# Dilated attention scores on four row groups of 32, and 512-wide pairs for the dilated chunks of the first layer

## The chip, the cores and the metric

The kernel runs on one core of one Trainium2 chip. Its time is the device time of one execution in microseconds (us); the median of the runs counts. Engines are named as the profile names them: PE (matmuls; PEld loads its weights), DVE (vector), ACT (scalar), POOL, and SP, whose queue issues the weight transfers.

## The reference

Two layers of a decoder trunk over 256 positions and a width of 1024, then a last normalization. Every layer runs one projection of the normalized input and three branches on its columns:

```
proj = hn @ w_in                      # a_q a_k a_v a_g | b_x b_g | c_q c_k c_v c_g
qa, ka = partial_rope(a_q), partial_rope(a_k)     # 8 heads of 64, the first 16 dims rotated
y_a = dilated_attention(qa, ka, a_v) * silu(a_g)  # three patterns: (128,1) (512,4) (2048,16)
y_b = rg_lru(b_x) * silu(b_g)                     # conv of 4, gates, linear recurrence
y_c = stick_breaking(c_q, c_k, c_v) * silu(c_g)   # 4 heads of 64
x = x + concat(y_a, y_b, y_c) @ w_out
```

In the dilated branch a query sees its causal keys, each with a weight that counts in how many patterns it occurs. Per head the scores are thus one 128x128 block (first query tile) and one 128x256 block (second query tile), with an additive mask.

## The kernel before

Activations are kept as two rounded parts, `xh` and `xl`, side by side in `xx`. The weights of a layer come in 18 chunks of 128x2048, two transfers each into `st`; ACT rounds each piece of 512 columns into `whi` (L109) and DVE puts the remainder into `wlo` (L110). A product is three matmul terms: hi by xh, hi by xl, lo by xh. A chunk of 256 output rows is made in two halves of 128 (`proj_b`). In the plain form (`mm3`, L211) each half is 24 matmuls 256 wide, and the two halves share one PSUM bank. In the paired form (chunks named in `PAIRED`, before in layer 1 alone) a half is 8 matmuls 512 wide (hi by xh and xl at once, L332) and 8 matmuls 256 wide (L329) in a PSUM bank of its own; ACT copies the xl half out (`low`, L335) and DVE adds it to the other (L337), which frees the bank.

PSUM has three pools: `pp` with three banks, `s` with four, `y` with one. `st` has five buffers.

Within a layer PE runs in the order in which the program is written; DVE, ACT and the others are ordered by a scheduler when the kernel is built. The order on PE in layer 0, from the stick-breaking queries on: CQ, CK, AQ0 (stick-breaking scores, L443, between its halves), AK0, BX (the convolution's input, with four transposes between its halves), eight more transposes (L463), AQ1 (between its halves `second`: the scores of dilated heads 0 to 3, L497), AK1, CG, twelve transposes of the probabilities (L463), BG (between its halves `third`: the recurrence's gates L557, the products with the values L427, the scores of heads 4 to 7), AG0, AG1, and the output chunks O0 to O3.

`rotate` applies the rotary table to a chunk's 512 columns with four DVE operations of that width (L481 to L484). `dil_scores` issues the fp32 matmuls of four heads, two heads at a time on 64 rows each, and then reads the scores on DVE (mask and minimum, L504). `dil_softmax` is an exponential per block on ACT (L83), a reciprocal (L515) and a scaling (L517) on DVE. `turned` copies transposed blocks from PSUM with ACT (L464, into `wv`, or `pa` and `pb`).

Of the kernel before, what the change touches and what calls it, by code (L numbers as in the profile page):

```python
# [20 lines left out]
NK = D // P  # L21
HD = 64
# [22 lines left out]
PAIRED = ((), (CH_CQ, CH_CK, CH_AQ[0], CH_AK[0], CH_BX, CH_AQ[1], CH_AK[1]))  # L45


@with_exitstack
def trunk_kernel(ctx: ExitStack, tc: tile.TileContext, x, first_x, first, wpack, prm_d, gatew, gains, consts, rope, out):
    nc = tc.nc  # L50
    act, dve, pe, gps = nc.scalar, nc.vector, nc.tensor, nc.gpsimd
# [35 lines left out]
    def v2(a, n=2):  # L87
        return a.rearrange("p (b t) -> p b t", b=n)
# [208 lines left out]
    for l in range(L):  # L297
# [8 lines left out]
        y_half(0)  # L306
# [7 lines left out]
        def proj_b(c, mid=None, to=None, sc=1.0):  # L314
            pair = c in PAIRED[l]
            hi, lo = [a.rearrange("p (k c) -> p k c", c=256) for a in weights(l, c, AHEAD - 1 if mid else AHEAD)]
            if pair:
                flat = None if to is not None else scr(512)
                to = v2(flat) if to is None else to
            else:  # L320
                flat = bank(pp, "pp")
            for b in range(2):
                cs = slice(b * P, b * P + P)
                if pair:
                    ps = bank(pp, "pp")
                    seq = [(0, k) for k in range(NK - 1)] + [(1, k) for k in range(NK)] + [(0, NK - 1)]
                    for i, (is_lo, k) in enumerate(seq):
                        if is_lo:
                            pe.matmul(ps[:, 0:S], lo[:, k, cs], xh[:, k, :], start=False, stop=False,  # L329
                                      skip_group_check=True)  # L330
                        else:
                            pe.matmul(ps, hi[:, k, cs], xx[:, k].rearrange("p h t -> p (h t)"), start=i == 0,  # L332
                                      stop=i == len(seq) - 1, skip_group_check=True)
                    low = wk.tile([P, S], F32, name="low", tag="low", bufs=2)
                    act.activation(low, ps[:, S:2 * S], AF.Copy, scale=sc)  # L335
                    if sc == 1.0:
                        dve.tensor_add(to[:, b, :], ps[:, 0:S], low)  # L337
                    else:
                        dve.scalar_tensor_tensor(to[:, b, :], ps[:, 0:S], sc, low, ALU.mult, ALU.add)
                else:  # L340
                    mm3(flat[:, b * 256:(b + 1) * 256], [lambda k, a=a: a[:, k, cs] for a in (hi, lo)],
                        [lambda k, a=a: a[:, k, :] for a in (xh, xl)], range(NK), True, True)
                if b == 0 and mid:
                    mid()
                    ask(l, c)
            return flat

        def proj_to(dst, c, mid=None, sc=1.0):
            if l > 0 and c in PAIRED[l]:
                proj_b(c, mid, dst, sc)  # L350
            else:
                scaled(dst, proj_b(c, mid), sc)

# [64 lines left out]
        def head(h):  # L418
            return slice((h % 2) * HD, (h % 2) * HD + HD), h // 2, slice(h * HD, (h + 1) * HD)
# [53 lines left out]
            parts[2] = a[:, 768:1024], b[:, 0:128]  # L473
            return parts

        def rotate(ps, tiles, h0, tag):
            dst = tiles[h0] = sb.tile([P, 2, S], F32, name=tag, tag=tag)
            rt_ = rp0 if l == 0 else rp
            cc, ss = [rt_[:, i:i + 1, :].broadcast_to([P, 2, S]) for i in range(2)]
            sw = scr(512)  # L480
            dve.stream_shuffle(sw, ps, SHUF)  # L481
            dve.tensor_mul(dst, v2(ps), cc)
            dve.tensor_mul(v2(sw), v2(sw), ss)
            dve.tensor_add(dst, dst, v2(sw))  # L484

        qT, kT = {}, {}
        prob = {}

        def dil_scores(h0):
            sps = {}  # L490
            for p in (h0, h0 + 2):
                for h in (p, p + 1):
                    sps[h] = bank(at, "s")
                for t, cs in halves:
                    for h in (p, p + 1):
                        hr, hb, _ = head(h - h0)
                        pe.matmul(sps[h][:, cs], qT[h0][hr, hb, t * P:(t + 1) * P], kT[h0][hr, hb, 0:(t + 1) * P],  # L497
                                  start=True, stop=True)
            shifted = {}
            for h in range(h0, h0 + 4):  # L500
                xs = scr(384)
                mn = wk.tile([P, 2], F32, name="mn", tag="mn", bufs=4)
                for t, cs in halves:
                    dve.tensor_tensor_reduce(xs[:, cs], sps[h][:, cs], nmask[:, cs], -0.125, 3e38,  # L504
                                             ALU.add, ALU.min, mn[:, t:t + 1])
                shifted[h] = xs, mn
            return shifted

        def dil_softmax(shifted):
            for h, (xs, mn) in shifted.items():  # L510
                pr = wk.tile([P, 384], F32, name="pr", tag="pr", bufs=4)
                den = wk.tile([P, 2], F32, name="den", tag="den", bufs=4)
                for t, cs in halves:
                    tab(pr[:, cs], xs[:, cs], AF.Exp, bias=mn[:, t:t + 1], scale=-1.0, accum_out=den[:, t:t + 1])
                dve.reciprocal(den, den)  # L515
                for t, cs in halves:
                    dve.tensor_scalar(pr[:, cs], pr[:, cs], den[:, t:t + 1], None, ALU.mult)  # L517
                prob[h] = pr
# [18 lines left out]
        ag = sb.tile([P, 4, S], F32, name="ag", tag="ag")  # L537
        cg = sb.tile([P, 2, S], F32, name="cg", tag="cg")

        def conv(mid):  # L540
# [53 lines left out]
        if l == 0:  # L594
            for i in range(2):
                dve.tensor_mul(rp0[:, i, :], rp[:, i, :], rb)
        rotate(proj_b(CH_AQ[0], sb_scores), qT, 0, "q0")
        rotate(proj_b(CH_AK[0]), kT, 0, "k0")
        sw_t, sw_heads = turned_tile()
        conv(lambda: turned(sw, 0, (0,), sw_t))  # L600
        turned(sw, 0, (1, 2), sw_t)
# [11 lines left out]
        silu(cg, cg_ps)  # L613


        def third():
            lru_gates()
# [7 lines left out]
        lru_scan()  # L625
        emit_y(rt, bg, 0, 2)
        dil_softmax(y_c["s"])
        ps = proj_b(CH_AG)
        table(SIGM)
        silu(ag[:, 0:2, :], ps)  # L630
# [56 lines left out]
def _rope_table():  # L687
    f = np.float32
    pos = np.arange(S, dtype=f)
    inv = f(500000.0) ** (-np.arange(0, 16, 2, dtype=f) / f(16))  # L690
    ang = (pos[:, None] * inv[None, :]).astype(f)
    cos, sin = np.cos(ang).T, np.sin(ang).T
    tab = np.zeros((P, 2, S), f)
    tab[:, 0] = 1.0
    for h in range(2):
        r = h * HD
        tab[r:r + 8, 0] = tab[r + 8:r + 16, 0] = cos
        tab[r:r + 8, 1] = -sin
        tab[r + 8:r + 16, 1] = sin
    return tab  # L700


def _pack_weights(w_in, w_out):
    wp = np.empty((L, NCH, P, 2048), np.float32)
    narrow = ((CH_CV, 3072), (CH_BX, 2048), (CH_BG, 2304), (CH_AG, 1536), (CH_AG + 1, 1792), (CH_CG, 3328),
              (CH_CQ, 2560), (CH_CK, 2816), (CH_AQ[0], 0), (CH_AQ[1], 256), (CH_AK[0], 512), (CH_AK[1], 768))
    yk = (4, 5, 6, 7, 0, 1, 2, 3)
    for l in range(L):
        wi = w_in[l].reshape(NK, P, 3584)
        for h in range(2):  # L710
            wp[l, CH_AV + h] = wi[4 * h:4 * h + 4, :, 1024:1536].transpose(1, 0, 2).reshape(P, 2048)
        for c, col in narrow:
            wp[l, c] = wi[:, :, col:col + 256].transpose(1, 0, 2).reshape(P, 2048)
# [62 lines left out]
```

## Time and profile before

| what | us |
|---|---|
| median of 3 runs (lowest to highest) | 249.79 (249.78 to 250.01) |
| the profiled execution | 248.82 |
| its span, first to last instruction | 246.7 |
| PE busy | 239.0 |
| DVE busy | 196.5 |
| ACT busy | 167.2 |

The profiled execution was 0.97 us shorter than the median, and 2.12 us of it lie outside the span. Positions in the trace are microseconds from the span's start. Layer 0's dilated chunks run from about 39 to 75, layer 1's from about 154 to 190. Rows of the timeline read: start, length, engine, line, operation, outputs and inputs, shape, number of instructions, and in brackets the idle time ahead with what ended it. Rows of the chain read: start, length, engine, tile, line, number.

### The profile page before, as it was taken

How to read it: one execution, taken by the hardware profiler on the slowest of the kernel's cores; microseconds unless marked ns; L12 is line 12 of the kernel's file. 1: busy time of each engine (PE TensorE's matmuls, PEld its weight loads, DVE VectorE, ACT ScalarE, POOL GpSimd, SP SyncE). 2: the span in 40 equal slices, each digit the busy share in tenths (PEclk: the TensorE clock that was granted, in tenths of full speed). 3: DMA queues.
4: the chain of work that ended last, by engine and by line, in shares of the span. 5: the costliest groups of instructions: out<-in, count | busy, mean ns of one | idle time of the engine just before them, and what ended most of it. 6: DMA issues, size and time to landing. Idle time of an engine off the chain costs nothing.

```text
span 246.7 us, 4531 instructions
## 1 busy us (share of the span) xinstructions
PE 239.0 (97%) x1657; PEld 212.1 (86%) x1657; DVE 196.5 (80%) x442; ACT 167.2 (68%) x360; POOL 12.1 (5%) x45
## 2 busy tenths in 40 slices
PE   8999999999999999999999999999999999999990
PEld 4889999999998899878889988889889889987870
DVE  3885699999999799985792766999999987985253
ACT  3778989735947499964662885865498649992142
POOL 0037000001000000000100000000010000000000
PEclk9999999999999999999999999999999999999998
DMA  6989889268447741277157486605553672000022
GB/s 201 404 292 403 342 288 333 96 215 268 134 157 255 258 117 56 85 240 284 74 189 232 142 268 243 200 7 165 161 157 119 197 262 98 0 0 3 0 85 85
DMA packets 13173, 43.89 MB, mean 178 GB/s; under 512 B 1632, under 2 KB 2144, under 8 KB 13152
## 3 DMA queue, kind: packets, MB, share of 16 engines
q1 hardware_dynamic: 12384, 42.30, 51.1%
q10 hardware_dynamic: 576, 0.79, 0.9%
q0 software_dynamic: 192, 0.52, 0.7%
q8 instruction: 13, 0.21, 0.4%
q14 instruction: 8, 0.07, 0.1%
HBM read 42.03 MB, written 1.05 MB: 175 GB/s over the span
## 4 chain that ended last, share of the span: by engine, by line
PE 94%; DMA 2%; DVE 1%; ACT 1%; SPq 0%; issue 0%; ACTq 0%
PE pp L211 51%; PE pp L332 11%; PE s L211 9%; PE pp L329 5%; PE s L169 4%; PE s L463 3%; PE s L497 2%; PE y L427 2%; DMA st<-first 2%; PE pp L169 2%; PE s L443 1%; PE pp L427 1%; PE s L557 1%; PE s L259 1%; DVE xres L668 0%; ACT scr L242 0%
## 5 line engine op out<-in xcount | busy, mean ns | idle before, releaser
L110 DVE TENSOR_TENSOR wlo<-st,whi 128x512 fp32r<-128x512 f32 x132 | 84.1, 683 | 12.8 <-ACT whi L109 12.5
L109 ACT ACTIVATE whi<-st 128x512 fp32r<-128x512 f32 x132 | 73.9, 629 | 28.0 <-PE pp L211 11.8
L211 PE MATMUL pp<-xx,whi 128*128 128x256 f32 x480 | 63.3, 285 | 0.0
L211 PEld LDWEIGHTS pp<-xx,whi 128*128 128x128 f32 x480 | 59.7, 191 | 1.4 <-issue 1.3
L211 PE MATMUL pp<-xx,wlo 128*128 128x256 f32 x240 | 33.7, 283 | 0.0
L211 PEld LDWEIGHTS pp<-xx,wlo 128*128 128x128 f32 x240 | 30.9, 192 | 0.0
L332 PE MATMUL pp<-xx,whi 128*128 128x512 f32 x112 | 29.3, 396 | 0.0
L332 PEld LDWEIGHTS pp<-xx,whi 128*128 128x128 f32 x112 | 20.1, 189 | 4.1 <-ACT scr L83 0.3
L77 ACT ACT_TABLE_LOAD x13 | 16.7, 1283 | 1.9 <-PEq L769 1.7
L83 ACT ACTIVATE pr<-scr,mn 128x128 f32<-128x128 f32 (+1 forms) x32 | 14.1, 442 | 5.2 <-DVE mn L504 5.2
L329 PEld LDWEIGHTS pp<-xx,wlo 128*128 128x128 f32 x112 | 15.3, 190 | 1.1
L329 PE MATMUL pp<-xx,wlo 128*128 128x256 f32 x112 | 15.6, 282 | 0.0
L211 PE MATMUL pp<-whi,yh 128*128 128x512 f32 x48 | 14.5, 403 | 0.0
L211 PE MATMUL pp<-wlo,yh 128*128 128x512 f32 x48 | 14.0, 393 | 0.0
L211 PE MATMUL pp<-whi,yl 128*128 128x512 f32 x48 | 14.0, 393 | 0.0
L335 ACT ACTIVATE low<-pp 128x256 f32<-128x256 f32 x14 | 5.3, 382 | 9.1 <-PE pp L332 6.8
L211 PEld LDWEIGHTS pp<-wlo,yh 128*128 128x128 f32 x48 | 9.0, 188 | 2.1
L211 PEld LDWEIGHTS pp<-whi,yl 128*128 128x128 f32 x48 | 9.0, 188 | 2.0
L211 PEld LDWEIGHTS pp<-whi,yh 128*128 128x128 f32 x48 | 8.6, 188 | 2.0 <-issue 0.3
L169 PE MATMUL s<-whi,xx 128*128 128x512 f32 (+1 forms) x36 | 10.2, 404 | 0.1
L415 ACT ACTIVATE yh<-scr 128x512 fp32r<-128x512 f32 x8 | 5.0, 631 | 7.7 <-DVE scr L413 7.6
L504 DVE CUSTOM_DVE_ANT_0 scr<-s,con 128x128 f32<-128x128 f32 (+1 forms) x32 | 9.2, 351 | 0.0
(165 smaller groups left out, 355.2 us busy)
## 6 DMA issues: line engine op xcount, KB each, us to landing
st<-w_pack SPq DMA_DIRECT2D x66, 512.0 KB, 5.4
st<-first SPq DMA_DIRECT2D x7, 512.0 KB, 6.2
xres<-x_in SPq DMA_DIRECT2D x2, 512.0 KB, 8.1
gw_t<-gate_w SPq DMA_DIRECT2D x2, 256.0 KB, 6.9
gn<-gains SPq DMA_DIRECT2D x1, 512.0 KB, 6.7
xs<-xc POOLq DMA_DIRECT2D x4, 128.0 KB, 3.7
gf<-gains SPq DMA_DIRECT2D x1, 512.0 KB, 6.8
out<-scr SPq DMA_DIRECT2D x2, 256.0 KB, 2.1
```

The lines of the kernel that those rows point to most:

```text
L77: load = act.preload_act_table_set(name)
L83: i = dep(act.activation(*a, **k), loaded["load"])
L109: split[l, c] = act.activation(hi[:, ws], st[:, ss], AF.Copy)
L110: dve.tensor_sub(lo[:, ws], st[:, ss], hi[:, ws].bitcast(F32))
L169: pe.matmul(ps[t][:, c0 - base:c1 - base], a[:, k, t * P:(t + 1) * P], b[:, c0:c1], start=k == 0 and i == 0 and c0 == base, stop=k == NK - ...
L211: pe.matmul(ps, a(k), b(k), start=first and i == 0, stop=last and i == len(seq) - 1)
L329: pe.matmul(ps[:, 0:S], lo[:, k, cs], xh[:, k, :], start=False, stop=False, skip_group_check=True)
L332: pe.matmul(ps, hi[:, k, cs], xx[:, k].rearrange("p h t -> p (h t)"), start=i == 0, stop=i == len(seq) - 1, skip_group_check=True)
L335: act.activation(low, ps[:, S:2 * S], AF.Copy, scale=sc)
L427: pe.matmul(y[hr, p * 128 + o:p * 128 + 256], vt[:, s0, hs], wts[i][s0], start=s0 == 0, stop=s0 == 1)
L463: pe.transpose(tp[:, i * P:(i + 1) * P], tiles[h0 + h][:, j * P:(j + 1) * P], ident)
L504: dve.tensor_tensor_reduce(xs[:, cs], sps[h][:, cs], nmask[:, cs], -0.125, 3e38, ALU.add, ALU.min, mn[:, t:t + 1])
```

## The change

The heads' columns in the chunks AQ and AK are packed on the host so that a head owns 32 rows in each of two parts: part 0 holds its first 32 dimensions, the rotated ones among them, and part 1 the other 32. Four heads then fill 128 rows.

- `rotated` takes the place of `rotate`: the rotary table is applied to part 0 alone (256 columns). In layer 1 part 1 is written where it belongs by the projection's own add; in layer 0 one multiply by `rb` (the row scale) does it.
- `split_qk` makes rounded parts of the second query tile and of the keys, each with a copy on ACT (L498) and a subtract on DVE (L499).
- `dil_scores` takes all four `s` banks at once. The first query tile is fp32 (8 matmuls), the second is three rounded terms (24 matmuls 256 wide), each over two parts of 32 rows and four heads (L513).
- `PAIRED[0]` names AQ0, AK0, AQ1 and AK1, so these chunks of layer 0 take the paired form.
- `y_half(0)` and `ag` are allocated later, and the splits reuse buffers of others by their tags.

```diff
-PAIRED = ((), (CH_CQ, ...
+PAIRED = ((CH_AQ[0], CH_AK[0], CH_AQ[1], CH_AK[1]), (CH_CQ, ...
...
-        def rotate(ps, tiles, h0, tag):
...
-            cc, ss = [rt_[:, i:i + 1, :].broadcast_to([P, 2, S]) for i in range(2)]
-            sw = scr(512)
-            dve.stream_shuffle(sw, ps, SHUF)
-            dve.tensor_mul(dst, v2(ps), cc)
-            dve.tensor_mul(v2(sw), v2(sw), ss)
-            dve.tensor_add(dst, dst, v2(sw))
+        def rotated(c, tiles, h0, tag, mid=None):
+            dst = tiles[h0] = sb.tile([P, 2, S], F32, name=tag, tag=tag)
+            tab_ = rp0 if l == 0 else rp
+            if l > 0:
+                src = scr(S)
+                proj_b(c, mid, [src, dst[:, 1, :]])
+            else:
+                ps = proj_b(c, mid)
+                src = ps[:, 0:S]
+            sh = scr(S)
+            dve.stream_shuffle(sh, src, SHUF)
+            dve.tensor_mul(dst[:, 0, :], src, tab_[:, 0, :])
+            dve.tensor_mul(sh, sh, tab_[:, 1, :])
+            dve.tensor_add(dst[:, 0, :], dst[:, 0, :], sh)
+            if l == 0:
+                dve.tensor_mul(dst[:, 1, :], ps[:, S:2 * S], rb)
...
+        def split_qk(h0, tags):
+            parts = []
+            for full, tag, n in ((qT[h0][:, :, P:S], tags[0], P), (kT[h0], tags[1], S)):
+                both = sb.tile([P, 2, 2, n], F32R, name="qk3", tag=tag)
+                act.activation(both[:, 0], full, AF.Copy)
+                dve.tensor_sub(both[:, 1], full, both[:, 0].bitcast(F32))
+                parts.append((both[:, 0], both[:, 1]))
+            (qh, ql), (kh, kl) = parts
+            exact[h0] = (qh, kh), (ql, kh), (qh, kl)
...
-            for p in (h0, h0 + 2):
-                for h in (p, p + 1):
-                    sps[h] = bank(at, "s")
-                for t, cs in halves:
-                    for h in (p, p + 1):
-                        hr, hb, _ = head(h - h0)
-                        pe.matmul(sps[h][:, cs], qT[h0][hr, hb, t * P:(t + 1) * P], kT[h0][hr, hb, 0:(t + 1) * P],
-                                  start=True, stop=True)
+            for h in range(h0, h0 + 4):
+                sps[h] = bank(at, "s")
+            for cs, n, terms in ((slice(0, P), P, ((qT[h0], kT[h0]),)), (slice(P, 384), S, exact[h0])):
+                seq = [(a, b, part) for part in range(2) for a, b in terms]
+                for i, (a, b, part) in enumerate(seq):
+                    for h in range(h0, h0 + 4):
+                        hr = slice(32 * (h - h0), 32 * (h - h0) + 32)
+                        pe.matmul(sps[h][:, cs], a[hr, part, 0:P], b[hr, part, 0:n],
+                                  start=i == 0, stop=i == len(seq) - 1)
...
-        rotate(proj_b(CH_AQ[0], sb_scores), qT, 0, "q0")
-        rotate(proj_b(CH_AK[0]), kT, 0, "k0")
+        rotated(CH_AQ[0], qT, 0, "q0", sb_scores)
+        rotated(CH_AK[0], kT, 0, "k0")
+        split_qk(0, ("yl0", "yh0"))
...
-        rotate(proj_b(CH_AQ[1], second), qT, 4, "q1")
-        rotate(proj_b(CH_AK[1]), kT, 4, "k1")
+        rotated(CH_AQ[1], qT, 4, "q1", second)
+        rotated(CH_AK[1], kT, 4, "k1")
+        split_qk(4, ("q0", "ag"))
```

The change also moves instructions on the engines that the scheduler orders. First PE in layer 0, from the first half of AQ1 on; the names behind `s<-` are keys and queries (`k_709`, `k_636`) and their rounded parts (`qk_`). Before:

```order
L211 MATMUL pp<-xx,whi 128x256 x16
L211 MATMUL pp<-xx,wlo 128x256 x8
L497 MATMUL s<-k_709,q_640 128x128 x2
L497 MATMUL s<-k_709,q_640 128x256 x2
L497 MATMUL s<-k_709,q_640 128x128 x2
L497 MATMUL s<-k_709,q_640 128x256 x2
L211 MATMUL pp<-xx,whi 128x256 x16
L211 MATMUL pp<-xx,wlo 128x256 x8
```

Now:

```order
L330 MATMUL pp<-xx,whi 128x512 x7
L327 MATMUL pp<-xx,wlo 128x256 x8
L330 MATMUL pp<-xx,whi 128x512
L513 MATMUL s<-k_636,q_525 128x128 x8
L513 MATMUL s<-qk_701,qk_698 128x256 x24
L330 MATMUL pp<-xx,whi 128x512 x7
L327 MATMUL pp<-xx,wlo 128x256 x8
```

Every place in PE's order is kept; the forms differ, and each half of a paired chunk now takes a bank of its own.

Second, DVE in layer 0 around the first softmax, before, from the convolution (`xc`) to AQ1's rotation:

```order
L544 TENSOR_SCALAR xc<-bxp,prm_t 128x256 x2
L546 SCALAR_TENSOR_TENSOR xc<-bxp,prm_t,xc 128x256 x6
L504 ISA scr,mn<-s,con 128x128
...
L517 TENSOR_SCALAR pr<-pr,den 128x256
L481 STREAM_SHUFFLE scr<-pp 128x512
L482 TENSOR_TENSOR q_929<-pp,rp_292 128x512
L483 TENSOR_TENSOR scr<-scr,rp_292 128x512
L110 TENSOR_TENSOR wlo<-st,whi 128x512
```

Now, from the convolution to the two adds (L335) that follow the softmax; the first of those belongs to AQ1's second half, the second to AK1's first half:

```order
L561 SCALAR_TENSOR_TENSOR xc<-bxp,prm_t,xc 128x256 x6
L335 TENSOR_TENSOR scr<-pp,low 128x256
L110 TENSOR_TENSOR wlo<-st,whi 128x512 x2
L485 TENSOR_TENSOR q_798<-scr,rp_292 128x256
L110 TENSOR_TENSOR wlo<-st,whi 128x512 x3
L520 ISA scr,mn<-s,con 128x128
...
L533 TENSOR_SCALAR pr<-pr,den 128x256
L335 TENSOR_TENSOR scr<-pp,low 128x256
L487 TENSOR_TENSOR q_798<-q_798,scr 128x256
L489 TENSOR_TENSOR q_798<-scr,rb 128x256
L110 TENSOR_TENSOR wlo<-st,whi 128x512
L335 TENSOR_TENSOR scr<-pp,low 128x256
```

The softmax (L520, before L504) stands behind five more wlo, an add and a multiply, and the add that empties the bank of AQ1's second half stands behind the softmax's last scaling.

Third, ACT in layer 0 from the end of the softmax's exponentials to the copies of the turned probabilities (`pa`). Before:

```order
L83 ACTIVATE pr,den<-scr,mn 128x256
L77 ACT_TABLE_LOAD
L109 ACTIVATE whi<-st 128x512 x11
L464 ACTIVATE pa<-s 128x512 x2
L464 ACTIVATE pb<-s 128x512
```

Now:

```order
L83 ACTIVATE pr,den<-scr,mn 128x256
L333 ACTIVATE low<-pp 128x256
L77 ACT_TABLE_LOAD
L333 ACTIVATE low<-pp 128x256
L109 ACTIVATE whi<-st 128x512 x2
L498 ACTIVATE qk_1003<-q_798 128x256
L109 ACTIVATE whi<-st 128x512 x2
L333 ACTIVATE low<-pp 128x256
L109 ACTIVATE whi<-st 128x512 x3
L498 ACTIVATE qk_1006<-k_941 128x512
L109 ACTIVATE whi<-st 128x512 x4
L462 ACTIVATE pa<-s 128x512 x2
```

Three copies `low` and two splits have come between the exponentials and `pa`; `pa` stands behind a row of `whi` as before.

More of the change, by code (lines that the diff above doesn't have):

```diff
@@ L44 @@
 CH_AQ, CH_AK = (5, 8), (6, 9)
-PAIRED = ((), (CH_CQ, CH_CK, CH_AQ[0], CH_AK[0], CH_BX, CH_AQ[1], CH_AK[1]))
+PAIRED = ((CH_AQ[0], CH_AK[0], CH_AQ[1], CH_AK[1]), (CH_CQ, CH_CK, CH_AQ[0], CH_AK[0], CH_BX, CH_AQ[1], CH_AK[1]))
 @with_exitstack
@@ L304, in y_half @@
             ys[h] = [sb.tile([P, 4, S], F32R, name=n, tag=f"{n}{h}") for n in ("yh", "yl")]
-        y_half(0)
         def proj_a(ps, w, t, kb, nk, cw, first, last):
@@ L318, in proj_b @@
                 flat = None if to is not None else scr(512)
-                to = v2(flat) if to is None else to
+                to = [v2(flat)[:, b, :] for b in range(2)] if to is None else to
             else:
@@ L336, in proj_b @@
                     if sc == 1.0:
-                        dve.tensor_add(to[:, b, :], ps[:, 0:S], low)
+                        dve.tensor_add(to[b], ps[:, 0:S], low)
                     else:
-                        dve.scalar_tensor_tensor(to[:, b, :], ps[:, 0:S], sc, low, ALU.mult, ALU.add)
+                        dve.scalar_tensor_tensor(to[b], ps[:, 0:S], sc, low, ALU.mult, ALU.add)
                 else:
@@ L349, in proj_to @@
             if l > 0 and c in PAIRED[l]:
-                proj_b(c, mid, dst, sc)
+                proj_b(c, mid, [dst[:, b, :] for b in range(2)], sc)
             else:
@@ L474, in by_head @@
             return parts
-        def rotate(ps, tiles, h0, tag):
+        def rotated(c, tiles, h0, tag, mid=None):
             dst = tiles[h0] = sb.tile([P, 2, S], F32, name=tag, tag=tag)
-            rt_ = rp0 if l == 0 else rp
-            cc, ss = [rt_[:, i:i + 1, :].broadcast_to([P, 2, S]) for i in range(2)]
-            sw = scr(512)
-            dve.stream_shuffle(sw, ps, SHUF)
-            dve.tensor_mul(dst, v2(ps), cc)
-            dve.tensor_mul(v2(sw), v2(sw), ss)
-            dve.tensor_add(dst, dst, v2(sw))
@@ L486, in trunk_kernel @@
-        qT, kT = {}, {}
-        prob = {}
+            tab_ = rp0 if l == 0 else rp
[10 more added lines that the diff above has]
+            dve.tensor_add(dst[:, 0, :], dst[:, 0, :], sh)
@@ new lines, in rotated @@
+            if l == 0:
+                dve.tensor_mul(dst[:, 1, :], ps[:, S:2 * S], rb)
+        qT, kT, exact = {}, {}, {}
+        prob = {}
+        def split_qk(h0, tags):
[7 more added lines that the diff above has]
+            exact[h0] = (qh, kh), (ql, kh), (qh, kl)
@@ L536, in trunk_kernel @@
         bg = sb.tile([P, 2, S], F32, name="bg", tag="bg")
-        ag = sb.tile([P, 4, S], F32, name="ag", tag="ag")
         cg = sb.tile([P, 2, S], F32, name="cg", tag="cg")
@@ L613, in trunk_kernel @@
         silu(cg, cg_ps)
+        y_half(0)
         def third():
@@ L627, in trunk_kernel @@
         dil_softmax(y_c["s"])
+        ag = sb.tile([P, 4, S], F32, name="ag", tag="ag")
         ps = proj_b(CH_AG)
@@ L694, in _rope_table @@
     tab[:, 0] = 1.0
-    for h in range(2):
-        r = h * HD
+    for r in range(0, P, 32):
         tab[r:r + 8, 0] = tab[r + 8:r + 16, 0] = cos
@@ L712, in _pack_weights @@
         for c, col in narrow:
-            wp[l, c] = wi[:, :, col:col + 256].transpose(1, 0, 2).reshape(P, 2048)
+            blk = wi[:, :, col:col + 256]
+            if c in CH_AQ + CH_AK:
+                blk = blk.reshape(NK, P, 4, 2, 32).transpose(0, 1, 3, 2, 4).reshape(NK, P, 256)
+            wp[l, c] = blk.transpose(1, 0, 2).reshape(P, 2048)
         wo = w_out[l].reshape(NK, P, D)
```

## The prediction

> **What bounds the kernel now.** I read the page first, then the chain of waits, then a table of busy time by stretches, then the timelines of PE, DVE and ACT where the change acts.
>
> ```profile
> PE 239.0 (97%) x1657; PEld 212.1 (86%) x1657; DVE 196.5 (80%) x442; ACT 167.2 (68%) x360; POOL 12.1 (5%) x45
> PE   8999999999999999999999999999999999999990
> DVE  3885699999999799985792766999999987985253
> PE 94%; DMA 2%; DVE 1%; ACT 1%; SPq 0%; issue 0%; ACTq 0%
> ```
>
> PE carries 94% of the chain and is full from the second slice to the last but one, so whatever shortens PE's work shortens the kernel, as long as nothing it waits for comes later. That condition is the question here: the DVE row shows nines where layer 0's dilated chunks run. The table by stretches (us, then PE, PEld, DVE, ACT, POOL busy, granted clock, DMA share, GB/s) sharpens it:
>
> ```profile
> 44.90:60.60 15.70, 15.70 (x136) 15.19 (x136) 15.70 (x32) 7.97 (x14) 0.41 (x4) 1.00 0.64 200
> 66.20:82.00 15.80, 15.80 (x152) 14.41 (x152) 15.72 (x29) 10.59 (x22) 0.00 (x0) 1.00 0.66 214
> 150.00:163.00 13.00, 13.00 (x82) 11.06 (x81) 10.01 (x21) 9.77 (x21) 0.00 (x0) 1.00 0.51 166
> ```
>
> In layer 0, from AQ0's rotation (44.9) to the softmax (60.6), DVE is busy 15.70 of 15.70 us; layer 1 has 10.01 of 13.00 early in the same stage. DVE in layer 0 costs nothing today only because PE needs its results later. The change gives it more to do there and makes PE need one result sooner.
>
> **The change part by part.** *Scores.* Each of four groups (two per layer) stands on the chain at 1.51 us:
>
> ```profile
> 57.72 1.51 PE s L497 x16
> 59.23 14.59 PE pp L211 x120
> 73.82 1.32 PE s L463 x12
> 75.14 2.87 PE pp L211 x24
> 78.01 1.02 PE s L557 x16
> ...
> 81.78 1.51 PE s L497 x16
> ```
>
> The 16 records are eight fp32 matmuls of two passes each, two heads side by side, two such pairs in turn. Per pair that is two passes 128 wide and two 256 wide, hence 12 units of 128 columns in all; 12 transposes of 128 columns take 1.32, or 0.11 a unit, so 1.3 us of the 1.51 is passes and 0.2 entry and exit. After: four heads side by side, tile 0 two parts of two passes (4 x 0.11 = 0.44), tile 1 six single-pass terms 256 wide (24 such in 2.87 us, 0.12 each: 0.72, or 0.65 by 0.109). With 0.2 around it: 1.3. I take −0.2 a group. This holds if four row groups run side by side, which no row of before shows for 32 rows; the nearest is the gates' 64x64 tiles:
>
> ```profile
> 77.94 0.43 PE L557 MATMUL s<-xc,gw_t 64*64 64x256 f32 x2
> 77.95 0.43 PE L557 MATMUL s<-xs,gw_t 64*64 64x256 f32 x2
> 78.21 0.38 PE L557 MATMUL s<-xc,gw_t 64*64 64x256 f32 x2
> ```
>
> Two and two start within 0.01 us: four at once. The ends: 1.1 (no entry or exit) and 2.5 (only two at once: 2 x 1.16 + 0.2), so −0.4 to +1.0 a group.
>
> *Pairs in layer 0.* An unpaired chunk-half and a paired one:
>
> ```profile
> 51.09 2.88 PE pp L211 x24
> 152.41 1.84 PE pp L332 x8
> 154.25 0.95 PE pp L329 x8
> ```
>
> 2.88 against 1.84 + 0.95 = 2.79: −0.09 a half, −0.18 a chunk, −0.7 for four. PE alone would gain 4 x 0.2 + 0.7 = 1.5.
>
> *Evictions.* Before, a chunk's two halves shared one PSUM bank, read later by the rotation. Now each half takes a bank of three and waits for ACT's `low` and DVE's add. CG's first matmul therefore takes the bank of AQ1's second half. The add that frees it stands on DVE, in the built order, behind the whole first softmax; before, CG needed only BX's bank. So the softmax's place on DVE now sets CG's start. DVE before:
>
> ```profile
> 44.91 0.74 DVE L481 STREAM_SHUFFLE scr<-pp 128x512 f32<-128x512 f32 x1
> 52.78 3.70 DVE L110 TENSOR_TENSOR wlo<-st,whi 128x512 fp32r<-128x512 f32 x6
> 58.24 2.46 DVE L546 SCALAR_TENSOR_TENSOR xc<-bxp,prm_t,xc 128x256 f32<-128x256 f32 x6
> 60.62 0.28 DVE L504 CUSTOM_DVE_ANT_0 scr<-s,con 128x128 f32<-128x128 f32 x1
> 64.48 0.28 DVE L515 RECIPROCAL den<-den 128x2 f32<-128x2 f32 x2
> 65.27 1.00 DVE L517 TENSOR_SCALAR pr<-pr,den 128x128 f32<-128x128 f32 x4
> 66.19 0.75 DVE L481 STREAM_SHUFFLE scr<-pp 128x512 f32<-128x512 f32 x1
> ```
>
> and the small add as layer 1 does it already (group view; starts in a row lie 0.335 apart, a 512-wide operation's 0.60):
>
> ```profile
> L337 DVE TENSOR_TENSOR scr<-pp,low 128x256 f32<-128x256 f32 x8 | 3.3, 418 | 0.0
> ```
>
> Between 44.9 and the softmax the order has, before: 12 wlo (7.2 us), two 512-wide rotations (4.9), `bxp` 0.6, the convolution 3.0. After: 16 wlo (9.6), the rotations at half width (1.7 each) with three adds (1.0), the splits' two subtracts (0.94), `bxp` and convolution (3.6), AQ1's first add and one multiply (0.67). That is 19.2 against 15.7. On top, DVE waits: k's subtract needs ACT's copy of k, which is queued behind `whi` copies that wait for DMA.
>
> ```profile
> 53.34 1.15 ACT L109 ACTIVATE whi<-st 128x512 fp32r<-128x512 f32 x2 [3.91 <-DMA st<-w_pack]
> 60.94 0.40 ACT L83 ACTIVATE pr<-scr,mn 128x128 f32<-128x128 f32 x1 [1.75 <-DVE mn L504]
> 64.38 0.19 ACT L83 ACTIVATION_READ_ACCUMULATOR pr<-scr,mn 128x1 f32 x1
> 64.58 1.28 ACT L77 ACT_TABLE_LOAD   x1
> 76.30 0.63 ACT L109 ACTIVATE whi<-st 128x512 fp32r<-128x512 f32 x1 [1.24 <-DMA st<-w_pack]
> 76.83 1.07 ACT L464 ACTIVATE pa<-s 128x512 f32<-128x512 f32 x2
> ```
>
> With the data of 53.3 the copy ends near 54.6, while DVE would be there at 53.8: 0.85 idle (ends 0 and 1.5). The softmax then starts at 44.85 + 19.2 + 0.85 = 64.95 instead of 60.62. ACT's eight exponentials paced it by 3.86 (60.62 to 64.48); reciprocals, the multiply put between and four scalings add 1.45, the add 0.35. `low` follows the last exponential and is ready by then. CG's bank is free at 64.95 + 3.86 + 1.45 + 0.35 = 70.6.
>
> When would PE be there? The quoted chain hides CG's start inside one piece; PE's timeline has it:
>
> ```profile
> 67.90 0.64 PE L211 MATMUL pp<-xx,whi 128*128 128x256 f32 x4
> ```
>
> 67.90 less 0.2 and 0.7 is 67.0; the scores now take all four "s" banks at once, and wait some 0.4 more for ACT to empty the last (`wv` copies of 0.53 like the `pa` row's, after PE's transposes), so 67.0 to 67.5. PE stalls 3.1 to 3.6 us, and CG starts 2.7 later than before: 70.6. The stall swallows every PE gain ahead of it.
>
> *What is late next.* The `pa` copies stand on ACT behind the last `whi` of a chunk whose transfer SP may issue only when a `st` buffer is free. That buffer's last reader is a wlo, which now runs after AK1's rotation, which runs after the softmax:
>
> ```profile
> 71.14 5.18 SPq L106 DMA_DIRECT2D st<-w_pack  x3
> st<-w_pack SPq DMA_DIRECT2D x66, 512.0 KB, 5.4
> ```
>
> Before, that transfer was issued at 71.14 and its `whi` began at 76.30, 5.16 later. After, ten operations 256 wide (0.34 each) and three wlo follow the 70.6, and that wlo ends near 75.8: `whi` at 81.0 with that landing, or at 79.7 if it is 1.3 shorter (my allowance: the DMA engines are busy 0.66 of that stretch, and the load is now spread later); the first `pa` copy is done 1.1 after. The gates need that bank. PE, 2.7 late, reaches them at 77.94 + 2.7 = 80.6; the copy is ready between 80.8 and 82.1. I take 82.0, since the quoted landing is the long one: gates 4.1 late. The second scores group gives back 0.2, and BG's second half starts 3.9 late. From there layer 0 follows PE: the `y` products have no earlier due time and the weights come ahead.
>
> *Layer 1* had its pairs already. DVE does less there (rotations on half width, −1.05 each, splits +0.94 a group), and the add before CG, already behind the softmax, ends some 0.3 before CG needs it, as before. Two groups give −0.4.
>
> *No price:* packing on the host, the two buffers allocated later, the table's rows (same size). Weight `whi`/`wlo` delays of up to 4 us in layer 0 are covered by chunks split two ahead; if that cover is gone, PE waits for `wlo` and the case is the upper end.
>
> *Sum:* +4.1 − 0.2 − 0.4 = +3.5 us. The profiled execution took 248.82 (span 246.7 and 2.12 around it), 0.97 under the median of 249.79. So 252.3 in such an execution, 253.3 as the median.
>
> In the trace of before PE has no gap above 0.3 us after its start, and the granted clock is 1.00 in every row of the table above. The Trainium skill, "TensorE: Matmul & The Clock Gate", section "Why this matters for your kernels", asks for no PE-idle gap over about 3 us, since one window of idle takes the clock back to half. By that rule the stall ahead of CG would cost more than its own length; the time it gives is the first rival's, 255.1 instead of 253.3. No run so far shows such a gap.
>
> **Rivals.**
>
> *Clock drop.* A forecast stall of 3.1 to 3.6 us is longer than any wait of PE before. The only hint of a cold array in the trace is PE's first work:
>
> ```profile
> L140 PE MATMUL y<-cold 128*128 128x512 bf16 x7 | 3.2, 630 | 1.2 <-DVE cold L128 1.2
> L332 PE MATMUL pp<-xx,whi 128*128 128x512 f32 x112 | 29.3, 396 | 0.0
> ```
>
> 630 ns against 396 for the same width. If PE came out of the stall so, CG's first 3 us of work would take 1.6 times as long: +1.8, to 255.1. DVE and ACT would catch up meanwhile, so part of the second stall goes; against it: 3.1 may be too short. This is the way that the rule of the Trainium skill above would take.
>
> *Row groups not concurrent.* At 2.5 us a group, three groups that are not hidden by the stall cost +1.2 each against my forecast: 256.9; at half of that 255.1. The gates' rows speak against it.
>
> *Faster.* CG's bank comes free in time. That takes an add done by 67.2, so a softmax that starts by 61.5 on DVE: 3.4 us less than my walk. It could be so if wlo rows that stand ahead in the built order wait less, and no 0.85 idle; but 19.2 us of DVE work cannot begin before the scans end at 44.85. Full gain: 249.79 − 1.5 = 248.3.
>
> *No change.* Without the idle 0.85, CG starts 1.85 late; with the shorter landing the gates do not wait; with scores at 1.1 the three groups after CG give back 1.2: +0.65, 250.4, and any 0.2 less of DVE work makes it "no change". With scores at 1.3 the same case gives 251.0. That the pairs themselves do nothing is excluded: layer 1's rows show both forms.
>
> **How the numbers follow.** About 0.2% (0.5 us) is what a measurement of this kernel can tell from no change. Chances: the two stalls as forecast, 250.9 to 254.5, 0.70; clock drop, 255.1, 0.09; row groups in turn, 255.1 to 256.9, 0.08; gain untouched, 248.3, 0.07; within 0.5 us of before, 0.06. Faster 0.07, same 0.06, slower 0.87. The likeliest is 253.3. The range runs from 250.9 (early landings, no idle) to 255.6 (clock drop, or half of the row-group loss), leaving out the fast cases (0.13) and the worst of the slow (0.06).
>
> **What would show it.** Right: PE idle for about 3 us ahead of CG (L211), released by DVE's add at L335; the first read of the scores (L520) near 65; a second, shorter wait at the gates (L572) on ACT's `pa`; score groups (L513) of about 1.3; layer 1 unchanged but for its scores. Wrong: CG following AK1 at once; L520 at 61 to 62; score groups above 1.5; gates without a wait; matmuls longer after the stall.

## The result, and the profile after

The changed kernel takes 253.42 us (four runs, 253.27 to 253.63) against 249.78 (249.77 to 250.01): 1.0146 times, with an interval of 1.0131 to 1.0161. The forecast was 253.3, slower, between 250.9 and 255.6. The time was right, its sum was not: of the two waits from which it was added up, one came and the other didn't, and a slow clock, a rival that had been given 9%, took its place.

The profiled execution took 253.63 (span 251.3). The same lines of the page as before, with the granted clock:

```profile
PE 240.7 (96%) x1689; PEld 210.9 (84%) x1689; DVE 196.0 (78%) x462; ACT 172.6 (69%) x376; POOL 11.1 (4%) x45
PE   7999999999869999999999999999999999999990
DVE  3874599999999688996495485899999967984253
PEclk9999999999979999999999999999999999999998
PE 82%; DVE 11%; ACT 2%; DMA 1%; issue 0%; SPq 0%; ACTq 0%
```

PE's share of the chain fell from 94% to 82%, DVE's rose from 1% to 11%. PE's row has a dent (an 8 and a 6), and in the second of these two slices the clock row has a 7. PE's own list of waits names the place, and the timeline shows it:

```profile
PE pp L211 <- DVE scr L335: 2.6, 1, 2.6
```

```profile
68.05 0.39 PE L330 MATMUL pp<-xx,whi 128*128 128x512 f32 x1
71.01 2.98 PE L211 MATMUL pp<-xx,whi 128*128 128x256 f32 x16 [2.58 <-DVE scr L335]
73.78 1.86 PE L211 MATMUL pp<-xx,wlo 128*128 128x256 f32 x8
75.48 2.06 PE L211 MATMUL pp<-xx,whi 128*128 128x256 f32 x16
82.61 0.43 PE L572 MATMUL s<-xc,gw_t 64*64 64x256 f32 x2
```

AK1 ends at 68.44, CG starts at 71.01, released by the add at L335. The first 16 matmuls of CG then take 2.98 us, the same 16 of its second half 2.06. The table by stretches (its seventh number, ahead of the DMA share, is the granted clock) says why:

```profile
68.40:71.00 2.60, 0.04 (x1) 0.00 (x0) 2.39 (x12) 2.57 (x7) 0.00 (x0) 1.00 0.01 3
71.00:72.00 1.00, 0.99 (x8) 0.99 (x9) 1.00 (x3) 1.00 (x3) 0.00 (x0) 1.00 0.00 0
72.00:73.00 1.00, 1.00 (x7) 1.00 (x7) 1.00 (x5) 1.00 (x4) 0.00 (x0) 0.53 0.09 25
74.00:75.00 1.00, 1.00 (x6) 1.00 (x6) 1.00 (x4) 1.00 (x3) 0.00 (x0) 0.50 0.86 246
75.00:76.00 1.00, 1.00 (x9) 1.00 (x8) 1.00 (x2) 1.00 (x3) 0.00 (x0) 0.77 0.23 94
```

One microsecond after PE resumes, the clock halves, and it stays so for 3.4 us (from 72.06 to 75.46, worked out from the 0.53 and the 0.77 of the rows at 72 and 75). In the chain CG's 48 matmuls stand at 7.50; in layer 1, where no wait precedes them, at 5.77:

```profile
71.01 7.50 PE pp L211 x48
189.89 5.77 PE pp L211 x48
```

So the clock costs 1.73. DVE and the score matmuls in the changed kernel:

```profile
58.42 0.73 PE L513 MATMUL s<-k,q 32*128 32x128 f32 x16
58.89 0.97 PE L513 MATMUL s<-qk,qk 32*128 32x256 f32 x24
54.93 0.69 DVE L499 TENSOR_TENSOR qk<-k,qk 128x512 fp32r<-128x512 f32 x1
65.24 0.28 DVE L520 CUSTOM_DVE_ANT_0 scr<-s,con 128x128 f32<-128x128 f32 x1
69.62 1.00 DVE L533 TENSOR_SCALAR pr<-pr,den 128x128 f32<-128x128 f32 x4
70.54 0.42 DVE L335 TENSOR_TENSOR scr<-pp,low 128x256 f32<-128x256 f32 x1
```

The first score group starts at 58.42 and the next matmul at 59.79: 1.37 instead of 1.51. At the gates (82.61) PE did not wait, since the first copy `pa` had ended near 81.1:

```profile
79.97 0.63 ACT L109 ACTIVATE whi<-st 128x512 fp32r<-128x512 f32 x1 [1.23 <-DMA st<-w_pack]
80.51 1.07 ACT L462 ACTIVATE pa<-s 128x512 f32<-128x512 f32 x2
```

The profiled executions differ by up to 1.7 us in what lies ahead of the dilated chunks (the stage below begins between 37.06 and 38.79), although every engine runs the same order over the first 34 us. I therefore compare a stage: from the first stick-breaking score matmul to the first matmul of BG's second half, just behind the second score group. In the profiles before it ran from 37.36 to 83.22, 45.9 us; after, from 38.47 to 87.76, 49.3: 3.4 more. What follows the stage lasts as long in both, 163.5 us. The 3.4 is 2.58 of waiting and 1.73 of slow clock, less 0.63 (seven paired halves) and 0.28 (two score groups).

### The profile page after: what moved, and what is told of

It reads as the page before. It is cut to its first block, busy times and chain, and to the rows that moved or that the text cites. A ratio compares the mean times of both kernels' runs of the same rounds, so it can differ in the third digit from the quotient of the medians.

```text
span 251.3 us, 4616 instructions
## 1 busy us (share of the span) xinstructions
PE 240.7 (96%) x1689; PEld 210.9 (84%) x1689; DVE 196.0 (78%) x462; ACT 172.6 (69%) x376; POOL 11.1 (4%) x45
## 4 chain that ended last, share of the span: by engine, by line
PE 82%; DVE 11%; ACT 2%; DMA 1%; issue 0%; SPq 0%; ACTq 0%
PE pp L211 40%; PE pp L330 11%; PE s L211 9%; PE pp L327 6%; PE s L169 5%; DVE wlo L110 4%; PE s L461 3%; PE pp L169 2%; PE y L425 2%; PE s L513 2%; DVE sw L452 1%; DMA st<-first 1%; ACT pr L83 1%; PE pp L425 1%; DVE xc L561 1%; PE s L572 1%
## 5 line engine op out<-in xcount | busy, mean ns | idle before, releaser
L211 PE MATMUL pp<-xx,whi 128*128 128x256 f32 x352 | 47.9, 289 | 2.6 <-DVE scr L335 2.6
L211 PEld LDWEIGHTS pp<-xx,whi 128*128 128x128 f32 x352 | 44.7, 194 | 3.9 <-DVE scr L335 2.9
L330 PE MATMUL pp<-xx,whi 128*128 128x512 f32 x176 | 46.3, 396 | 0.0
L330 PEld LDWEIGHTS pp<-xx,whi 128*128 128x128 f32 x176 | 31.6, 189 | 6.2 <-issue 0.3
L327 PEld LDWEIGHTS pp<-xx,wlo 128*128 128x128 f32 x176 | 24.0, 190 | 1.8
L211 PE MATMUL pp<-xx,wlo 128*128 128x256 f32 x176 | 25.4, 289 | 0.0
L327 PE MATMUL pp<-xx,wlo 128*128 128x256 f32 x176 | 24.5, 282 | 0.0
L211 PEld LDWEIGHTS pp<-xx,wlo 128*128 128x128 f32 x176 | 23.5, 198 | 0.0
L333 ACT ACTIVATE low<-pp 128x256 f32<-128x256 f32 x22 | 8.4, 383 | 5.9 <-PE pp L330 5.8
L520 DVE CUSTOM_DVE_ANT_0 scr<-s,con 128x128 f32<-128x128 f32 (+1 forms) x32 | 9.2, 351 | 0.0
```

What stands on the lines that cost most here:

```text
L211: pe.matmul(ps, a(k), b(k), start=first and i == 0, stop=last and i == len(seq) - 1)
```

## The experiments

Theory A: one PSUM bank makes the loss. CG waits for an add that stands behind the softmax, and the idle time lowers the clock. Rivals: DVE's extra work in layer 0 makes it, wherever the bank is (B); the pairs alone make it (C); the clock falls for another reason (D). "Stage" is the stretch defined above, from each run's profile, which is one execution; ratios are to the kernel before, with their intervals. A loss inside a score group, at the gates or at O0 is what that place takes more than without a wait.

| kernel | median us | ratio | stage us | PE's new waits in layer 0 |
|---|---|---|---|---|
| before | 249.9 to 250.0 | 1 | 45.9 | none |
| the change | 253.42 | 1.0146 (1.0131 to 1.0161) | 49.3 | CG 2.6, then half clock |
| scores alone | 249.48 | 0.9979 (0.9961 to 0.9998) | 46.2 | inside the first score group 0.6 |
| pairs alone | 251.36 | 1.0062 (1.0047 to 1.0077) | 46.6 | inside the first score group 1.2; O0 0.5 |
| change, gap filled | 252.05 | 1.0086 (1.0070 to 1.0102) | 47.8 | CG as before (filled) |
| change, add ahead | 251.81 | 1.0076 (1.0056 to 1.0095) | 47.8 | CG 0.6, gates 1.9 |
| three pairs | 250.72 | 1.0029 (1.0011 to 1.0046) | 46.6 | gates 1.4 |
| three pairs, copies ahead | 253.00 | 1.0106 (1.0077 to 1.0134) | 47.6 | second score group 2.4 |
| add ahead, copies ahead | 251.76 | 1.0072 (1.0047 to 1.0097) | 47.5 | first score group 0.5, CG 0.2, second score group 1.6 |
| fp32 second tile | 251.87 | 1.0093 (1.0061 to 1.0125) | 47.6 | CG 2.1 |
| three pairs, gates ahead | 250.61 | 1.0026 (1.0009 to 1.0043) | 45.2 | none in the stage; O0 1.3 |
| two pairs, gates ahead | 250.64 | 1.0029 (1.0010 to 1.0048) | 45.3 | none in the stage; O0 1.3 |
| before, gates ahead | 251.13 | 1.0052 (1.0035 to 1.0069) | 45.9 | none in the stage; O0 1.1 |
| scores alone, copies ahead | 248.66 | 0.9959 (0.9943 to 0.9975) | 45.6 | none |

**The two parts apart.** The scores alone:

```diff
-PAIRED = ((CH_AQ[0], CH_AK[0], CH_AQ[1], CH_AK[1]), (CH_CQ, ...
+PAIRED = ((), (CH_CQ, ...
```

> The new scores without layer 0's pairs. Theory A (the loss is one PSUM bank: CG waits for AQ1's second add, which stands behind the first softmax, and the idle time then lowers the clock): CG needs BX's bank again, no wait of PE, no low clock; four score groups at 1.37 instead of 1.51 give 0.56: 249.2. Rival B (the loss is DVE's overload: the splits push the softmax back, whatever the bank): the softmax starts near 62.4 instead of 60.6, and PE waits later, at the turned probabilities or at the gates: 250.3 or more.

A gain of 0.48 us, where theory A gave 0.56, without a wait at CG and without a fall of the clock. DVE began the softmax 2.6 later than before, counted from the stage's start (63.81 - 37.99 against 60.62 - 37.36), and PE waited for it nowhere, which speaks against B. But the profile does not show the gain either: it has a loss of 0.6 at another place, inside the first score group (2.0 us), of which below; its stage is 0.3 longer than before, and what follows lasts 163.6. So this profile does not explain the 0.48, and where it lies no run shows. The pairs alone put the same `PAIRED` into the kernel before:

> Layer 0's pairs with the old scores and rotations. In its order too the add of AQ1's second half stands behind the softmax. Theory A, by DVE's durations: 15.85 us of DVE work stand between the scans and the softmax (19.2 in the whole change), so the softmax starts near 61, the add is done near 67.5 and PE is there near 67.2: a wait of 0.2 to 0.7 without a fall of the clock, 249.78 - 0.7 + 0.2 to 0.7 = 249.3 to 249.8. Rival C (the pairs with three banks are the whole loss, wherever the softmax is): a wait of over 2 us, a low clock and 252.5 or more.

251.36 lies between the two, and the expected wait did not come: PE reached CG late, because it had waited before, in the middle of the first score group, for ACT to copy turned blocks out of the banks.

```profile
58.36 0.93 PE L497 MATMUL s<-k,q 64*128 64x128 f32 x8
59.73 1.41 PE L497 MATMUL s<-k,q 64*128 64x128 f32 x8 [0.44 <-ACT wv L464]
```

The group took 2.70 instead of 1.51. C falls as it was stated (no clock fall, 251.4 instead of 252.5), but so does my place: the pairs alone cost time through ACT's queue, not through CG's bank. The large loss needs both parts together.

**The clock.** The gap filled with matmuls that nobody reads:

```diff
+        if l == 0:
+            fill = bank(yp, "y")
+            for _ in range(10):
+                pe.matmul(fill, xh[:, 0, 0:P], xx[:, 0].rearrange("p h t -> p (h t)"), start=True, stop=True)
         cg_ps = proj_b(CH_CG)
```

> The whole change with ten unused 512-wide matmuls on PE between AK1 and CG of layer 0, which fill the 2.6 us in which PE is idle. Theory A with the clock (the idle time lowers the clock for 3.4 us of work after it): the granted clock stays 1.00, CG's 48 matmuls take 5.8 instead of 7.5: 1.7 less, 251.7; if the gates then wait for ACT's copies of the turned probabilities, which were ready 0.65 after PE would come, 252.3. Rival D (the clock falls at this place for another reason): CG takes 7.5 as before, 253.4.

PE worked on the fill from 68.46 and started CG at 71.09, as late as before; but the stretch in which the clock had been at half reads

```profile
72.00:74.00 2.00, 2.00 (x19) 2.00 (x18) 2.00 (x8) 2.00 (x6) 0.00 (x0) 1.00 0.22 74
```

and the stage is 1.5 shorter. The idle time lowers the clock (D falls), and this costs 1.5 of the 3.6 us.

The second query tile in fp32, without the splits, shortened the gap to 2.07:

```diff
-            for cs, n, terms in (..., (slice(P, 384), S, exact[h0])):
+            for cs, n, terms in (..., (slice(P, 384), S, ((qT[h0][:, :, P:S], kT[h0]),))):
...
-        split_qk(0, ("yl0", "yh0"))
...
-        split_qk(4, ("q0", "ag"))
```

> The whole change, but the second query tile is fp32 like the first (two parts of 32 rows, 8 matmuls instead of 24) and the rounded parts are not made. On PE: four fp32 passes of 0.215 instead of six rounded of 0.109 a group, 1.58 instead of 1.37, +0.8 in four groups. On DVE: the splits' subtracts (0.94) go, one more wlo moves ahead of the softmax: it starts 0.3 earlier, PE comes 0.2 later, so the wait at CG is near 2.0 instead of 2.6. If the clock still falls after 2.0 us of idle time: 253.4 - 0.3 + 0.6 = 253.7. If it doesn't: 252.0.

Both times came. Four of six executions took 251.7 to 251.9 with a mean clock of 0.994 or 0.995, two took 253.3 and 253.7 at 0.989. In the profiled one the clock held:

```profile
70.45 2.17 PE L211 MATMUL pp<-xx,whi 128*128 128x256 f32 x16 [2.07 <-DVE scr L335]
```

A gap of 2.6 lowered the clock in the change's profiled run; its other three runs took the same time within 0.4 us, and their mean clocks (0.987 and 0.988) lie below those of the kernel before (0.991 to 0.998). By the same two signs the clock fell in two of these six executions with a gap of about 2.1; neither of the two was profiled. The first fp32 score group took 1.53, against 1.37 with the three rounded terms: the rounding saves 0.16 a group on PE, and the four row groups on 32 rows alone save nothing against 1.51.

**The place of one add.** The copies `low` and the adds of layer 0 raised in the scheduler's order:

```diff
-                    low = wk.tile(...)
-                    act.activation(low, ps[:, S:2 * S], AF.Copy, scale=sc)
...
+                    with tc.high_priority() if l == 0 else nullcontext():
+                        low = wk.tile(...)
+                        act.activation(low, ps[:, S:2 * S], AF.Copy, scale=sc)
...
```

> The whole change, with layer 0's copies low and adds raised in the scheduler's order, so that the add that frees CG's bank stands between the second and third head's scaling instead of behind the last. Theory A alone: the add is done near 68.9 in the frame of the changed kernel's trace instead of 70.9, PE waits 0.5 instead of 2.6 and the clock stays up: 253.4 - 2.0 - 1.7 = 249.7. Theory A with the second wait of the prediction (the copies of the turned probabilities come no earlier, since ACT still waits for the transfer of O0): PE waits some 2 us at the gates, 251.5 to 252. Rival B (the late softmax itself): no gain, 253.4.

The wait at CG fell to 0.63, and the clock held. What I had forecast as the second wait now came: PE stopped at the gates for ACT's copies `pa`, which stood behind a split that waited for O0's transfer.

```profile
68.65 2.18 PE L211 MATMUL pp<-xx,whi 128*128 128x256 f32 x16 [0.63 <-DVE scr L336]
80.73 0.43 PE L573 MATMUL s<-xs,gw_t 64*64 64x256 f32 x2 [1.31 <-ACT pa L463]
79.56 0.63 ACT L109 ACTIVATE whi<-st 128x512 fp32r<-128x512 f32 x1 [2.43 <-DMA st<-w_pack]
80.10 1.06 ACT L463 ACTIVATE pa<-s 128x512 f32<-128x512 f32 x2
```

From 78.78, where the gates begin, to the values at 81.74 it is 2.96 us instead of 1.02: 1.9 of the 3.7 regained were lost again. A without the second wait (249.7) falls, A with it (251.5 to 252) stands at 251.81.

Three pairs give CG a bank that is free in time:

```diff
-PAIRED = ((CH_AQ[0], CH_AK[0], CH_AQ[1], CH_AK[1]), (CH_CQ, ...
+PAIRED = ((CH_AQ[0], CH_AK[0], CH_AQ[1]), (CH_CQ, ...
```

> The whole change with AK1 of layer 0 unpaired: CG then takes the bank of AQ1's first half, which is freed ahead of the softmax. The softmax stands where it stood in the whole change. Theory A: no wait at CG and no fall of the clock; three pairs and the scores give 0.54 + 0.56; at the gates PE comes early and waits for the copies of the turned probabilities as in the run with the add ahead (1.9 lost there), here 0.3 to 1.7: 249.2 to 250.6. Rival B (the late softmax itself holds layer 0): PE waits at the turned probabilities for the softmax, 252 or more.

No wait at CG, the softmax where it was, 2.7 us less than the change: the late softmax costs nothing at CG when PE's bank does not hang on it. B falls in this form. The gates took 1.4 too long:

```profile
79.50 0.43 PE L572 MATMUL s<-xs,gw_t 64*64 64x256 f32 x2 [0.75 <-ACT pa L462]
```

Here something of B remains: O0's transfer, for which `pa` waited, was issued at 73.66, when a wlo behind the late softmax had freed its buffer. Counted from the stage's start that is 1.8 later than the 71.14 of before.

**Taking away the second wait.** O0's splits of layer 0 put behind the copies (`dep` puts its first instruction behind its second on the same engine), once with three pairs and once with the add ahead:

```diff
+    copies = []
...
                 split[l, c] = act.activation(hi[:, ws], st[:, ss], AF.Copy)
+                if (l, c) == (0, CH_O):
+                    dep(split[l, c], copies[-1])
...
-                act.activation(to[g], tp, AF.Copy)
+                copies.append(act.activation(to[g], tp, AF.Copy))
```

> As the run with three pairs, and ACT splits O0 of layer 0 only after it has copied the turned probabilities, so that these copies no longer wait for O0's transfer. Theory A with the second wait: no wait of PE at CG nor at the gates, 249.96 - 0.54 - 0.56 = 248.9. If the second wait has another cause (the transposes' own readiness, say), the same time as with three pairs alone.

> The whole change with all four pairs, the add for CG's bank ahead in the order (251.81 alone), and the turned probabilities' copies ahead of O0's splits. Theory A with the second wait: the 1.9 us lost at the gates come back, the 0.6 at CG stay: 249.9. If the wait at the gates was not for O0's transfer: 251.8.

Both expectations failed by 2 to 4 us. The gates no longer waited, so O0's transfer was their cause; but the splits now ran ahead of the gates' sigmoids (`rt`, `it`), which empty two banks of the second score group. Three pairs, PE and then ACT:

```profile
83.97 0.48 PE L516 MATMUL s<-k,q 32*128 32x128 f32 x2 [1.20 <-ACT rt L83]
80.48 0.63 ACT L83 ACTIVATE scr<-scr 128x512 f32<-128x512 f32 x1 [2.78 <-DVE scr L393]
81.02 2.18 ACT L110 ACTIVATE whi<-st 128x512 fp32r<-128x512 f32 x4
83.10 0.82 ACT L83 ACTIVATE rt<-s,prm_t 128x256 f32<-128x256 f32 x2
```

The first of these rows on ACT is CG's sigmoid, which itself waited 2.78 for DVE. Four of the six executions with three pairs took 252.9 to 253.3 at a mean clock of 0.989 to 0.991, the profiled one 251.73 at 0.995: here too the wait probably lowered the clock in some, though no profile of such a one exists.

So the sigmoids too: O0's splits and CG's sigmoid behind the gates' sigmoids, in three kernels, one of them the control.

```diff
+    gated = []
...
+                if (l, c) == (0, CH_O):
+                    dep(split[l, c], gated[-1])
...
-            tab(sg, src, AF.Sigmoid)
+            gate = tab(sg, src, AF.Sigmoid)
+            if behind is not None:
+                dep(gate, behind)
...
-                    tab(dst[:, b, :], ...)
+                    gated.append(tab(dst[:, b, :], ...))
...
-        silu(cg, cg_ps)
+        if l > 0:
+            silu(cg, cg_ps)
...
+            if l == 0:
+                silu(cg, cg_ps, gated[-1])
```

> Three pairs in layer 0 (AK1 unpaired), and on ACT the copies of the turned probabilities and the gates' four sigmoids stand ahead of O0's splits and of CG's sigmoid, which waits for DVE. Theory A' (PE loses only where it meets a result that stands on ACT or DVE behind work that is late; in layer 0 these places are CG's bank, the copies of the turned probabilities, the gates' sigmoids): none of the three holds PE, 249.95 - 0.54 - 0.56 = 248.9. Rival B (DVE's extra work in layer 0 makes the time, and each cure only moves the wait): the time of the runs with one cure, 250.7 or more, with a wait at a new place.

> As the run with three pairs and the gates ahead, but with two pairs (AQ0, AK0) and the wv copies ahead of BG's splits. Theory A': 249.95 - 0.36 - 0.56 = 249.0. Rival B: as there, 250 or more.

> The kernel before, with the same order on ACT (gates' sigmoids ahead of O0's splits and CG's sigmoid) and nothing else: the control. The kernel before has no wait of PE at these places, so the order alone should gain nothing: 249.7 to 250.2. If it gains over 0.5, the gain of the other runs is not the change's.

(The two pairs also have the copies ahead of BG's splits, as below.) Inside the stage the change now gives all that it can: 45.2 with three pairs, where 45.9 less five halves of 0.09 and two groups of 0.14 is 45.1. But all three lose at O0, whose first product waits for ACT's `yh`; three pairs, then the control:

```profile
99.45 1.20 PE L214 MATMUL s<-whi,yh 128*128 128x512 f32 x4 [1.12 <-ACT yh L418]
```

```profile
100.12 1.20 PE L214 MATMUL s<-whi,yh 128*128 128x512 f32 x4 [0.97 <-ACT yh L420]
```

My expectation of the control (no difference) was wrong by 1.2 us, and the control shows whose loss that is: the order's, not the change's. Against the control, three pairs and the scores are 0.5 us faster, and 0.7 in the stage alone.

**The best version.** The scores alone, with BG's splits behind the `wv` copies that empty the banks of the first score group:

```diff
+                if (l, c) == (0, CH_BG):
+                    dep(split[l, c], copies[-1])
...
-                act.activation(to[g], tp, AF.Copy)
+                copies.append(act.activation(to[g], tp, AF.Copy))
```

> The new scores without layer 0's pairs (249.48 before, with 0.6 lost inside the first score group), and ACT copies the turned weights (wv), which empty the banks of that score group, ahead of BG's splits that wait for a transfer. Theory A': the first group takes 1.37 instead of 2.0 and nothing else changes: 248.9. Rival B: PE waits at a later place instead, 249.5.

ACT without this order, then ACT and the score group with it:

```profile
57.28 0.63 ACT L109 ACTIVATE whi<-st 128x512 fp32r<-128x512 f32 x1 [0.91 <-DMA st<-w_pack]
57.82 1.06 ACT L462 ACTIVATE wv<-s 128x512 f32<-128x512 f32 x2
```

```profile
54.16 1.08 ACT L465 ACTIVATE wv<-s 128x512 f32<-128x512 f32 x2 [0.38 <-PE s L464]
57.35 0.73 PE L516 MATMUL s<-k,q 32*128 32x128 f32 x16
57.82 0.97 PE L516 MATMUL s<-qk,qk 32*128 32x256 f32 x24
```

The group takes 1.37, nothing waits later, and the time is 248.66: 0.9959 of the kernel before, faster than both kernels. Here the cure moved no wait, so B falls in its second form too (each cure only moves the wait): it depends on what else the moved splits are put in front of. The trace explains only a part of the gain: the stage is 0.3 shorter (two score groups), and what follows it lasts 163.6 instead of 163.5. About 1 of the 1.26 us lies elsewhere, perhaps ahead of the stage, where executions differ most; no run shows what makes it.

## Why the prediction was right, point by point

- **Scores.** Forecast 0.2 a group, measured 0.14. The range's upper end (row groups in turn, 2.5 a group) did not come; the term was mis-sized by a third. I had put it down to four row groups side by side; the fp32 run (1.53) shows that the rounded terms carry it.
- **Pairs in layer 0.** 0.09 a half as forecast: the three-pair run with no wait left has the stage of the sum.
- **DVE's walk.** Forecast: softmax at 64.95 (its three terms add up to 64.90). Taken back by the 1.11 us by which this execution's stage began later, it started at 64.13. The idle 0.85 in front of k's subtract was the part that failed: ACT's copy was ready at 54.90, and the subtract started at 54.93 behind the wlo ahead of it. Without that term the walk is exact to 0.1.
- **The wait at CG.** Forecast 3.1 to 3.6, measured 2.58. Taken back by the same 1.11, the bank was free at 69.9 instead of 70.6 (the missing 0.85 again), and PE was there at 67.3, within the forecast 67.0 to 67.5. The cause, the add behind the softmax, is shown by the run with the add ahead and by three pairs.
- **The second wait, at the gates.** Forecast +1.4, measured none. The step that failed first is "I take 82.0, since the quoted landing is the long one". Taken back by 1.11, ACT's split of O0 began at 78.9 instead of 81.0 and the first `pa` copy ended near 80.0: the 0.85 was missing here too, and the transfer, issued at 76.22, needed 3.7 instead of 5.16. CG at half clock did the rest: PE came at 81.5 instead of 80.6. But the clock alone does not decide it. With the gap filled the clock stayed up, CG started as late, and the gates took 1.03, without a wait. The wait came (1.9 long) in the run with the add ahead, where PE was 3.4 earlier at the gates and O0's split began at 78.9, as here.
- **The clock.** Given as a rival at 9% and 1.8 us; it came, and cost 1.73 by the profile. That the sizes agree is luck: the rival had 3 us of work at 1.6 times its length, the trace has half the clock for 3.4 us, and the first matmuls, from which the 1.6 was taken, ran at a granted clock of 1.00. The reason against it ("3.1 may be too short") was wrong: 2.58 is enough. The Trainium skill, "TensorE: Matmul & The Clock Gate", section "Why this matters for your kernels", sets the limit at about 3 us of idle time. The trace differs: an idle 2.58 lowered the clock, and some 2.1 did in two of six executions by their times and mean clocks; the measurement decides. That the clock is halved agrees (0.50).
- **Sum.** Forecast +3.5 with 4.1 at the gates and 0.6 given back later; measured +3.64. At the gates PE was 82.61 − 77.94 − 1.11 = 3.6 late, 0.5 less than forecast: an overlong first wait and a second wait that was absent, against a clock fall that was left out. That the total agrees to 0.1 us is luck: these errors cancel.
- **Layer 1.** Forecast −0.4. The two score groups gave 0.28, but the output products of both layers are slower by some 0.2 each (in layer 0 from O0's start to the next twelve matmuls from `yh` and `yl`, 102.42 to 116.56 in the chain, 14.14, where before it was 97.89 to 111.83, 13.94), so nothing was left. The chains of all kernels made from the changed one have this; why was not tried.

## What to carry to other kernels

When a result that PE needs moves behind a long block in the built order of another engine, PE waits for what is left of that block when it gets there; count which reader frees the next PSUM bank, and where that reader stands in the built order, before counting matmuls saved. A copy that empties a bank must not stand behind work that waits for a transfer; but each reordering pushes something else back, so run the reordering on the old kernel as a control. A change with two parts is worth measuring by its parts: here one part with one changed order on ACT measured 0.4% faster, with most of that not explained by the trace, and the whole lost 1.5%.

## What was not expected of the hardware

After 2.58 us of idle time PE's granted clock fell not at once but 1.0 us after PE had resumed, to 0.50 for 3.4 us. After some 2.1 us of idle time it held in the profiled execution, and by time and mean clock it fell in two of six: whether it falls differs there from execution to execution. Ten unused matmuls in the gap of 2.6 kept it at 1.00.
